# RWKV-7 decode samples: loads one pair of heads ahead, masks and half of the group norms on VectorE

## The chip, the cores and the metric

The kernel runs on one core of one Trainium2 chip. The metric is the device time of one launch in microseconds (us). TensorE (PE) does the matmuls, VectorE (DVE) and ScalarE (ACT) the elementwise work, GpSimd (POOL) a few copies and products, SyncE (SP) issues most of the DMAs. Each engine takes its instructions in order; what is late on one holds everything written behind it on that engine.

## What the reference computes

One step of a two-layer decoder: a gated-DeltaNet mixer and a ConvFFN, then an RWKV-7 mixer and a ConvFFN. The same trunk runs for a prompt (16 meta tokens and 512 tokens) and for 8 samples of 4 tokens that start from given states. The change lies in the RWKV mixer, cut here to what it computes (16 heads of 64):

```
def rwkv_step(S, xs):
    r_t, w_t, k_t, v_t, kk_t, a_t = xs
    sa = einsum('bhvk,bhk->bhv', S, kk_t)
    S = S * w_t - sa[..., None] * (kk_t * a_t) + v_t[..., None] * k_t
    y = einsum('bhvk,bhk->bhv', S, r_t)
    return S, y

S, y = lax.scan(rwkv_step, S0, (r, decay, k, v, kk, a))
mu = mean(y, axis=-1); var = mean(square(y - mu), axis=-1)
y = ((y - mu) * rsqrt(var + GN_EPS)) * ln_w + ln_b      # a norm per head and token
y = y + sum(r * k * r_k) * v                            # bonus
out = (y * gate) @ wo
```

## The kernel before

All 560 tokens (32 of the samples, 528 of the prompt) are columns of one activation matrix; the model width of 1024 is 8 tiles of 128 rows. A product with a weight matrix is done in fp32 by three matmuls of split halves (`hi`, `lo`: L70 on ACT and L71 on DVE split the weights, L115 multiplies).

The recurrence is done in chunks of 64 tokens: products of a chunk's keys (L1353, mask L1360 on DVE), inverses of 32x32 blocks (L1404 to L1418) and their merging (`merge`, 32x32 matmuls L1443 and L1448 with ACT copies L1444 and L1449), then `rec(G)`, which carries the state through the chunks. The 16 heads are two halves, G = 0 and 1, of four pairs of heads each. In a chunk of `rec`, PE, ACT and DVE take turns: L1624 and L1628 on PE, L1629 on ACT, L1633 on PE, L1565 on DVE, L1642 on PE, L1644 on DVE, L1577 on ACT, and L1651 with L1652 for the outputs. SP loads the keys and values of chunk c+2 (L1572, L1573) when chunk c is done. After every second chunk comes `outnorm`, the norm per head: a sum (L1671, DVE), eight ACT operations of 64 columns that take the mean off (L1674), a square (L1676, ACT), a sum (L1677, DVE), an inverse square root of ten small DVE operations, eight ACT operations of 64 columns that scale (L1681), transposes on PE (L1685) and two finishing operations on DVE (L1690, L1691). Each half has six such norms: one for the meta tokens, four for the prompt, one for the samples.

`samples(G)` does the 8 samples for the four pairs of half G, one pair after the other (q = 0 to 3), in one set of buffers: `S0b` (states, for L1739), `S0` (the state to be updated), `vt`, `vx` and `kt` (tokens). Per pair: the loads (L1717 to L1724) and POOL copies (L1731, L1732), then PE L1739 and L1738, ACT L1740, PE L1744, DVE L1565, PE L1749, DVE L1750, two ACT copies (L1752), eight ACT operations that multiply `vx` by a sample's indicator (L1754, the masks), PE L1757, DVE L1758, POOL L1759 and the store (L1760).

`gates` is the gating product, in two halves of 280 columns and 8 tiles each (loads L1535 and L1537, splits L1538 on ACT and L1541 on DVE, matmuls L1547 and L1548, ACT L1549, DVE L1550). The output product has two halves too: `out_half` for G = 0 (tile `osA`, L115; loads of `xs` L1784, sum L1786, store L1787), and the half for G = 1 (`osB`), which comes after all norms and is split by L183 and L184.

The order of all this is set by `Weave`: chains (samples, rec, norms, inverses) and slots (large products, `gates`, `out_half`, in sequence, each behind a gate). A step ends at a `yield a, b, n`: the planner's clock moves by a, and the chain may go on b later. Chains come first; a slot's step is taken when no chain is due. So the yields set the order in which instructions of different chains stand on each engine.

Of the kernel before, what the change touches and what calls it, by code (L numbers as in the profile page):

```python
# [11 lines left out]
AF = mybir.ActivationFunctionType  # L12
# [5 lines left out]
P = 128  # L18
# [1032 lines left out]
def rwkv(E, xp, norm, x_dram, sink):  # L1051
# [4 lines left out]
    with st:  # L1056
# [609 lines left out]
        def outnorm(G, Yt, r, o, n, t, room, lock):  # L1666

            hp = slice(4 * G, 4 * G + 4)
            y = Yt[r].rearrange("p a (u d) -> p (a u) d", u=2)
            mu, var, rs = [ar.tile([P, 8], F32, tag=g, name=g, bufs=2) for g in ("gm", "gv", "gr")]  # L1670
            nc.vector.tensor_reduce(mu[r], y, axis=AX.X, op=ALU.add)  # L1671
            nc.vector.tensor_scalar(mu[r], mu[r], -1.0 / 64.0, None, op0=ALU.mult)
            for u in range(8):
                nc.scalar.activation(y[:, u], y[:, u], AF.Identity, bias=mu[r, u:u + 1])  # L1674
            sq = room[r]
            nc.scalar.activation(sq, Yt[r].rearrange("p a (u d) -> p a u d", u=2), AF.Square)  # L1676
            nc.vector.tensor_reduce(var[r].rearrange("p (a u) -> p a u", u=2), sq, axis=AX.X, op=ALU.add)  # L1677
            nc.vector.tensor_scalar(var[r], var[r], 1.0 / 64.0, 64e-5, op0=ALU.mult, op1=ALU.add)
            rsqrt(E, ar, rs[r], var[r], [P, 8], "gs", r)
            for u in range(8):  # L1680
                nc.scalar.activation(y[:, u], y[:, u], AF.Copy, scale=rs[r, u:u + 1])  # L1681
            yield 0, 6.0, 0
            py = bank([4, n])
            for p in range(4):
                nc.tensor.transpose(py[:, p, :], Yt[r, p, :], E.ident[r, r])  # L1685
            vo, go = v[:, hp, o:o + n], G1[:, hp, o:o + n]
            if n == P:
                py, vo, go = [x.rearrange("p a (c t) -> p a c t", c=2) for x in (py, vo, go)]
            def finish(y):
                nc.vector.tensor_tensor(t, y, go, op=ALU.mult)  # L1690
                nc.vector.tensor_tensor(vo, t, vo, op=ALU.add)  # L1691
            if gated:
                finish(py)
            else:
                nc.scalar.activation(t, py, AF.Copy)
                pending.append(lambda: finish(t))
            if lock is not None:
                ylock[lock] = False
            normed[G] += 1
            yield 0.45, 0.5, 1  # L1700

        def samples(G):
# [9 lines left out]
            nc.gpsimd.memset(kt, 0.0)  # L1712
            nc.gpsimd.memset(vt[up], 0.0)

            def load(p):
                for r in (dn, up):
                    nc.sync.dma_start(out=S0b[r, :, r], in_=I["rwkv_S0"][p, r])  # L1717
                nc.sync.dma_start(out=S0, in_=I["rwkv_S0"][p])
                nc.sync.dma_start(out=vt[dn], in_=vtd[0, :, p, :])
                for hh, c in enumerate((dn, up)):  # L1720
                    nc.sync.dma_start(out=vx[64 * hh:64 * hh + 32], in_=vtd[0, 0:32, p, c])
                    for i in range(2):
                        o = 64 * hh + 32 * i
                        nc.sync.dma_start(out=kt[o:o + 32, c], in_=kbd[0, 64 * i:64 * i + 32, p, c])  # L1724
            for q in range(4):
                p = 4 * G + q
                load(p)
                for i in range(2):
                    x = KR[:, p, 0, i, 0:32].rearrange("p (b t) -> p b t", t=4)
                    zo = 64 * i  # L1730
                    nc.gpsimd.tensor_copy(z[:, zo:zo + 924].rearrange("p (b c) -> p b c", c=132)[:, :, 0:4], x[:, 0:7])  # L1731
                    nc.gpsimd.tensor_copy(z[:, zo + 924:zo + 928], x[:, 7])  # L1732
                yield 0, 2.5, 0
                ps = bank([P])
                for k in range(8):
                    if k == 7:
                        for hh, c in enumerate((dn, up)):
                            nc.tensor.matmul(ps[b, c], lhsT=Ak[dn, 2 * q + hh, 0:32], rhs=vt[dn, c], start=False, stop=False)  # L1738
                    nc.tensor.matmul(ps, lhsT=z[:, P * k:P * k + P], rhs=S0b[:, k, :], start=(k == 0), stop=(k == 7))  # L1739
                nc.scalar.activation(PY, ps, AF.Copy)  # L1740
                yield 2.1, 0.8, 1
                ps = bank([1, P])
                for hh, c in enumerate((dn, up)):
                    nc.tensor.matmul(ps[b, 0, c], lhsT=Ak[b, 2 * q + hh, 0:32], rhs=PY[b, c], start=True, stop=True)  # L1744
                evac_SA(vt[b].unsqueeze(1), ps[b], b, 0, 2 * p, 2)
                yield 0.15, 1.0, 1
                ps = bank([P])
                for hh, c in enumerate((dn, up)):
                    nc.tensor.matmul(ps[a, c], lhsT=Ar[:, 2 * q + hh, 0:32], rhs=vt[:, c], start=True, stop=True)  # L1749
                nc.vector.tensor_tensor(ys[a, q, :], ps[a], PY[a], op=ALU.add)  # L1750
                for hh, c in enumerate((dn, up)):
                    nc.scalar.activation(vx[64 * hh + 32:64 * hh + 64], vt[b, c], AF.Copy)  # L1752
                for b8 in range(8):
                    nc.scalar.activation(vm[:, b8], vx, AF.Copy, scale=ind[:, b8:b8 + 1])  # L1754
                yield 0.15, 1.5, 1
                ps = bank([8, 64])
                nc.tensor.matmul(ps, lhsT=kt, rhs=vm, start=True, stop=True)  # L1757
                nc.vector.tensor_tensor(S0, S0, ps, op=ALU.add)  # L1758
                nc.gpsimd.tensor_tensor(S0, S0, el[:, p, 0:8].unsqueeze(2).to_broadcast([P, 8, 64]), op=ALU.mult)  # L1759
                nc.sync.dma_start(out=O["rwkv_Ss"][p], in_=S0)  # L1760
                yield 0.86, 0.5, 1
            W.chain(outnorm(G, ys, a, 0, 32, KR[:, 4 * G:4 * G + 4, 0, 0, 0:32],
                            f[:, 0:512].rearrange("p (a u d) -> p a u d", a=4, u=2), None))
# [15 lines left out]
        def out_half():  # L1779
            ot = split_half(0, big(E, F32R, "osA", 0))  # L1780
            for m in range(KD):
                t = E.xp.tile([P, T], F32, tag="s", name="xs", bufs=2)[:, :TG]
                for a, b in last_cols(t, x_dram[m]):
                    nc.sync.dma_start(out=a, in_=b)  # L1784
                ps = yield from dense_g(E, [4], ot, TG // 2, n=TG)
                nc.vector.tensor_tensor(half_cols(t), ps[:, :, :TG // 2], half_cols(t), op=ALU.add)  # L1786
                nc.sync.dma_start(out=x2[m], in_=t)  # L1787
# [6 lines left out]
        def seconds():  # L1794
            for i, (r, f) in enumerate(((dn, ev_a), (up, ev_w))):
# [4 lines left out]
        W.slots += [[None, slot(ev_r(m), hook=making(3) if m == 7 else None, split=304)] for m in range(KD)]  # L1800
        W.slots += [[None, slot(ev_v(m))] for m in range(KD)]
        W.slots += [[None, products2()], [lambda: all(ktdone) and len(zdone) == KD and prod_done[1], gates()],
                    [lambda: normed[0] == 6 and bool(gated) and bool(merged[1]), out_half()]]
        W.run()
        assert normed == [6, 6]
        stA.close()
# [233 lines left out]
```

## Time and profile before

| | |
|---|---|
| device time, median of 3 runs (lowest, highest) | 1912.06 us (1908.01, 1916.1) |
| the profiled execution: device time, its span in the trace | 1913.3 us, 1911.3 us |
| mean granted TensorE clock of it | 0.95 of full |
| busy: PE, DVE, ACT, POOL | 1801.1, 1154.5, 803.9, 369.0 us |

Busy time is the union of an engine's instructions. The granted clock is 1.00 at TensorE's full clock of 2.4 GHz and 0.50 at 1.2 GHz; a mean between the two is a share of time at either. The time outside the span is 2.0 us.

### The profile page before, as it was taken

The numbers are of one execution on the slowest core, as the hardware profiler recorded it, in microseconds if no ns is written. First come the engines' busy times: TensorE is split into PE (matmuls) and PEld (weight loads), VectorE is DVE, ScalarE is ACT, GpSimd is POOL, SyncE is SP. The second block draws the span as 40 slices with busy tenths as digits, with TensorE's granted clock in tenths as the row PEclk, the third lists the DMA queues.
The fourth block names the chain that finished last, engine by engine and source line by source line (L and its number), as shares of the span: only waits on it lengthen the run. The fifth ranks groups of instructions, "written<-read, shape, count | busy, mean of one in ns | idle before, by whom it ended". The sixth has DMA issues, their size and how long they took to land.

```text
span 1911.3 us, 36670 instructions
## 1 busy us (share of the span) xinstructions
PE 1801.1 (94%) x14673; PEld 1718.5 (90%) x14673; DVE 1154.5 (60%) x2221; ACT 803.9 (42%) x1779; POOL 369.0 (19%) x616
## 2 busy tenths in 40 slices
PE   7999999999999999998989999799997999999996
PEld 6889998789999999998778997788786999999996
DVE  6698973875555553337787977874555555554223
ACT  4766434442222222222976535554644322222221
POOL 3442403621222220013110000021001111111011
PEclk9999998999999999999898999896898999999998
DMA  4233232433222223444122244332235322223331
GB/s 131 76 91 93 70 90 104 150 122 120 82 89 89 80 87 104 120 155 98 48 70 62 70 117 121 98 91 80 78 102 163 123 89 89 89 88 91 99 109 67
DMA packets 128010, 186.13 MB, mean 97 GB/s; under 512 B 63088, under 2 KB 75376, under 8 KB 127840
## 3 DMA queue, kind: packets, MB, share of 16 engines
q10 hardware_dynamic: 34448, 111.63, 18.7%
q1 hardware_dynamic: 93392, 72.17, 13.0%
q8 instruction: 116, 1.90, 0.4%
q14 instruction: 54, 0.44, 0.1%
HBM read 151.56 MB, written 32.18 MB: 96 GB/s over the span
## 4 chain that ended last, share of the span: by engine, by line
PE 76%; DVE 12%; ACT 3%; DMA 3%; issue 1%; POOL 0%; SPq 0%; DVEq 0%; ACTq 0%
PE pd L115 56%; PE pd L138 3%; PE pg L1353 1%; DVE lo L71 1%; PE pg L1739 1%; PE pg L1628 1%; DVE it L425 1%; PE pg L1624 1%; PE pg L1651 1%; PE pg L1642 1%; DVE tri L1023 1%; PE pg L835 1%; PE pg L1633 1%; DVE cv L593 1%; DMA xd<-xo 1%
## 5 line engine op out<-in xcount | busy, mean ns | idle before, releaser
L115 PE MATMUL pd<-x,hi 128*128 128x280 f32 (+7 forms) x4768 | 837.5, 297 | 23.5 <-ACT hi L70 9.1
L115 PEld LDWEIGHTS pd<-x,hi 128*128 128x128 f32 (+1 forms) x4768 | 695.4, 192 | 30.8 <-ACT hi L70 9.3
L115 PE MATMUL pd<-x,lo 128*128 128x296 f32 (+5 forms) x2384 | 516.4, 297 | 5.6 <-DVE lo L71 5.6
L70 ACT ACTIVATE hi<-raw 128x1024 fp32r<-128x1024 f32 (+3 forms) x218 | 219.8, 1009 | 481.7 <-PE pd L115 447.4
L115 PEld LDWEIGHTS pd<-x,lo 128*128 128x128 f32 (+1 forms) x2384 | 382.9, 192 | 9.9 <-DVE lo L71 6.8
L71 DVE TENSOR_TENSOR lo<-raw,hi 128x1024 fp32r<-128x1024 f32 (+3 forms) x218 | 255.7, 1173 | 219.1 <-ACT hi L70 212.6
L218 POOL TENSOR_TENSOR s<-s,sq 128x560 f32<-128x560 f32 (+2 forms) x30 | 50.8, 1693 | 303.7 <-ACT sq L216 273.9
L304 DVE TENSOR_TENSOR gp<-pd,s 128x528 f32<-128x528 f32 (+1 forms) x44 | 30.8, 701 | 105.9 <-PE pd L115 105.9
L115 PE MATMUL pd<-hl,hi 128*128 128x280 f32 (+1 forms) x448 | 93.5, 290 | 0.0
L115 PE MATMUL pd<-hh,hi 128*128 128x280 f32 (+1 forms) x448 | 93.3, 290 | 0.0
L115 PE MATMUL pd<-hh,lo 128*128 128x280 f32 (+1 forms) x448 | 93.3, 290 | 0.0
L316 ACT ACTIVATE gs<-cv 128x528 f32<-128x528 f32 (+1 forms) x44 | 28.1, 639 | 147.3 <-DVE cv L314 147.3
L115 PE MATMUL pd<-hb,hi 128*128 128x280 f32 (+1 forms) x512 | 85.8, 290 | 0.0
L115 PEld LDWEIGHTS pd<-hb,hi 128*128 128x128 f32 x512 | 72.8, 188 | 0.0
L115 PEld LDWEIGHTS pd<-hh,lo 128*128 128x128 f32 x448 | 70.8, 188 | 0.0
L115 PEld LDWEIGHTS pd<-hh,hi 128*128 128x128 f32 x448 | 70.6, 188 | 0.0
L115 PEld LDWEIGHTS pd<-hl,hi 128*128 128x128 f32 x448 | 70.5, 188 | 0.0
L319 POOL TENSOR_TENSOR gs<-gs,s 128x560 f32<-128x560 f32 (+1 forms) x44 | 60.8, 1382 | 38.1 <-ACT gs L317 38.1
L322 DVE TENSOR_TENSOR h<-pd,gs 128x560 f32<-128x560 f32 (+1 forms) x44 | 32.1, 730 | 57.0 <-POOL gs L319 57.0
L308 POOL COPY fnew<-gp 128x2 f32<-128x2 f32 x44 | 8.1, 185 | 291.5 <-DVE gp L304 291.5
L1023 DVE TENSOR_TENSOR tri<-X 128x4 f32<-128x4 f32 (+26 forms) x124 | 56.0, 451 | 5.2 <-POOL X L1014 2.2
L138 PE MATMUL pd<-os,hi 128*128 128x280 f32 x256 | 52.8, 303 | 2.5 <-ACT os L183 1.9
(539 smaller groups left out, 3039.6 us busy)
## 6 DMA issues: line engine op xcount, KB each, us to landing
raw<-w_up ACTq DMA_DIRECT2D x88, 512.0 KB, 3.3
raw<-w_in ACTq DMA_DIRECT2D x32, 512.0 KB, 3.3
raw<-w_down ACTq DMA_DIRECT2D x32, 512.0 KB, 3.6
raw<-w_down ACTq DMA_DIRECT2D x16, 384.0 KB, 3.0
kbd<-kst SPq DMA_DIRECT2D x18, 256.0 KB, 2.0
KB<-kbd SPq DMA_DIRECT2D x18, 256.0 KB, 3.0
xd<-xo SPq DMA_DIRECT2D x16, 280.0 KB, 2.1
raw<-gdn_out ACTq DMA_DIRECT2D x8, 512.0 KB, 3.3
```

The costliest lines, as they stand in the source:

```text
L70: nc.scalar.activation(hi[:R, :kt, :M], raw[:R, :kt, :M], AF.Copy)
L71: lo_eng.tensor_tensor(lo[:R, :kt, :M], raw[:R, :kt, :M], hi[:R, :kt, :M].bitcast(F32), op=ALU.subtract)
L115: nc.tensor.matmul(ps[b][:M, :c1 - c0] if isinstance(ps, list) else ps[:M, b, :c1 - c0], lhsT=w[:, kk, :M], rhs=x[:, c0:c1], start=(k == 0 ...
L138: nc.tensor.matmul(ps[:, b, :c1 - c0], lhsT=a, rhs=x[:, c0:c1], start=(k == i == 0), stop=(k == len(xs) - 1 and i == 2))
L218: nc.gpsimd.tensor_tensor(self.acc[:, :self.w], self.acc[:, :self.w], sq, op=ALU.add)
L304: nc.vector.tensor_tensor(two(gp[:, m0:]), pm, two(s[:, mo:mo + ml]), op=ALU.mult)
L316: nc.scalar.activation(gs[:, mo:mo + ml], cv[:, m0 - 2:], AF.Silu)
L319: nc.gpsimd.tensor_tensor(gs, gs, s[:, :n_main], op=ALU.mult)
L322: nc.vector.tensor_tensor(two(h), ps[:, :, :hw], two(gs), op=ALU.mult)
L425: nc.vector.tensor_tensor(t.rearrange("p n j -> p j n"), U[:n, i:R, c0:], L[:n, i, i:R].unsqueeze(2).to_broadcast([n, m, k]), op=ALU.mult)
L593: nc.vector.scalar_tensor_tensor(cv, gp[:, i:i + 584], cw[i], cv, op0=ALU.mult, op1=ALU.add)
L1023: nc.vector.tensor_tensor(t.rearrange("p n j -> p j n"), X[:n, i + 1:c1, c0:c1], X[:n, i, i + 1:c1].unsqueeze(2).to_broadcast([n, m1, k]), ...
```

## The change

The samples of a pair no longer load everything at the pair's start. `load` is cut into three: the states (L1717 with the POOL copies), the tokens, and the own state `S0`. For the first pair of a half all three run together, with one `yield 0, 2.5, 0` for the half and none for the others; for the next pair the states are loaded behind the first PE group of the pair before (its readers), the tokens behind L1757 and `S0` behind the store. The eight ACT masks become one DVE operation of 512 columns. In `outnorm`, for G = 1 only, the eight ACT operations for the mean and the eight for the scale become one DVE operation of 512 columns each; G = 0 keeps its ACT operations. The gate of `out_half` no longer asks that all inverses of half 1 are merged. Nothing in the arithmetic changes.

```diff
             nc.vector.tensor_scalar(mu[r], mu[r], -1.0 / 64.0, None, op0=ALU.mult)
-            for u in range(8):
-                nc.scalar.activation(y[:, u], y[:, u], AF.Identity, bias=mu[r, u:u + 1])
+            if G:
+                nc.vector.tensor_tensor(y, y, mu[r].unsqueeze(2).to_broadcast([r.stop - r.start, 8, 64]), op=ALU.add)
+            else:
+                for u in range(8):
+                    nc.scalar.activation(y[:, u], y[:, u], AF.Identity, bias=mu[r, u:u + 1])
...
-            for u in range(8):
-                nc.scalar.activation(y[:, u], y[:, u], AF.Copy, scale=rs[r, u:u + 1])
+            if G:
+                nc.vector.tensor_tensor(y, y, rs[r].unsqueeze(2).to_broadcast([r.stop - r.start, 8, 64]), op=ALU.mult)
+            else:
+                for u in range(8):
+                    nc.scalar.activation(y[:, u], y[:, u], AF.Copy, scale=rs[r, u:u + 1])
...
-            def load(p):
+            def load_states(p):
+
                 for r in (dn, up):
                     nc.sync.dma_start(out=S0b[r, :, r], in_=I["rwkv_S0"][p, r])
-                nc.sync.dma_start(out=S0, in_=I["rwkv_S0"][p])
...
+            def load_tokens(p):
                 nc.sync.dma_start(out=vt[dn], in_=vtd[0, :, p, :])
...
+            def load_own(p):
+                nc.sync.dma_start(out=S0, in_=I["rwkv_S0"][p])
+            for f_ in (load_states, load_tokens, load_own):
+                f_(4 * G)
+            yield 0, 2.5, 0
             for q in range(4):
                 p = 4 * G + q
-                load(p)
...
-                yield 0, 2.5, 0
...
                 nc.scalar.activation(PY, ps, AF.Copy)
+                if q < 3:
+                    load_states(p + 1)
                 yield 2.1, 0.8, 1
...
-                for b8 in range(8):
-                    nc.scalar.activation(vm[:, b8], vx, AF.Copy, scale=ind[:, b8:b8 + 1])
+                nc.vector.tensor_tensor(vm, vx.unsqueeze(1).to_broadcast([P, 8, 64]), ind.unsqueeze(2).to_broadcast([P, 8, 64]), op=ALU.mult)
                 yield 0.15, 1.5, 1
                 ps = bank([8, 64])
                 nc.tensor.matmul(ps, lhsT=kt, rhs=vm, start=True, stop=True)
+                if q < 3:
+                    load_tokens(p + 1)
                 nc.vector.tensor_tensor(S0, S0, ps, op=ALU.add)
...
                 nc.sync.dma_start(out=O["rwkv_Ss"][p], in_=S0)
+                if q < 3:
+                    load_own(p + 1)
                 yield 0.86, 0.5, 1
...
-                    [lambda: normed[0] == 6 and bool(gated) and bool(merged[1]), out_half()]]
+                    [lambda: normed[0] == 6 and bool(gated), out_half()]]
```

PE's order is the same in both kernels up to the first L1757 of half 0, and again from the second half of the output product on. In between, three places matter. The line numbers of the changed kernel are higher: L1739 is L1751 there, L1744 L1758, L1757 L1770, L1685 L1691, L1718 L1740, L1717 L1724, L1719 L1732, L1721 L1734, L1724 L1737, L1760 L1775, L1784 L1801, L1787 L1804.

The first place is PE where the first half of the output product begins; XX and A are the buffers of the samples of half 0 and 1, KB and KR belong to the recurrence. Before:

```order
L1739 MATMUL pg<-A 128x128 x7
L1738 MATMUL pg<-A 32x64 x2
L1739 MATMUL pg<-A 128x128
L1633 MATMUL pg<-KB,A 64x64 x8
L1685 MATMUL pg<-cm,XX 128x32 x4
L1744 MATMUL pg<-A 32x64 x2
L1642 MATMUL pg<-KB 128x128 x4
L1651 MATMUL pg<-KB,A 64x64 x8
L115 MATMUL pd<-osA,hi 128x274 x2
L1624 MATMUL pg<-KB,KR 128x128 x4
```

And with the change:

```order
L1751 MATMUL pg<-A 128x128 x7
L1750 MATMUL pg<-A 32x64 x2
L1751 MATMUL pg<-A 128x128
L1633 MATMUL pg<-KB,A 64x64 x8
L1691 MATMUL pg<-cm,XX 128x32 x4
L1758 MATMUL pg<-A 32x64 x2
L1642 MATMUL pg<-KB 128x128 x4
L1651 MATMUL pg<-KB,A 64x64 x6
L115 MATMUL pd<-osA,hi 128x274
L1651 MATMUL pg<-KB,A 64x64 x2
L115 MATMUL pd<-osA,hi 128x274 x5
L1624 MATMUL pg<-KB,KR 128x128 x4
```

Both times the output product begins right behind the norm of half 0's samples (the L1685, now L1691, that reads XX); but the L1624 that follows is that of rec(1)'s last chunk, the eighth, before, and that of its sixth chunk now, so that three chunks stand between the output product's matmuls.

The second place is PE at the end of that half. Before:

```order
L1685 MATMUL pg<-cm,KB 128x128
L1757 MATMUL pg<-A 128x512
L1685 MATMUL pg<-cm,KB 128x128 x3
L115 MATMUL pd<-osA,hi 128x274 x4
L115 MATMUL pd<-osA,lo 128x274 x2
...
L115 MATMUL pd<-osB,hi 128x274 x2
L1685 MATMUL pg<-cm,A 128x32 x4
L115 MATMUL pd<-osB,hi 128x274 x5
```

And with the change:

```order
L115 MATMUL pd<-osA,hi 128x274 x4
L1642 MATMUL pg<-KB 128x128 x4
L1651 MATMUL pg<-KB,A 64x64 x8
L1770 MATMUL pg<-A 128x512
L115 MATMUL pd<-osA,lo 128x274 x2
L115 MATMUL pd<-osA,hi 128x274 x4
...
L1691 MATMUL pg<-cm,KB 128x128 x4
L115 MATMUL pd<-osB,hi 128x274 x2
L1691 MATMUL pg<-cm,A 128x32 x4
L115 MATMUL pd<-osB,hi 128x274 x5
```

The end of the last chunk (its L1642 and L1651) stands some 20 matmuls of the output product ahead of osB now; before, it stood ahead of nearly all of the output product. The last norm's transposes are the next thing behind those matmuls.

The third place is SP's queue in rec(1), where pairs of half 1 (A) are loaded between the recurrence's loads (KB). Before:

```order
L1572 DMA KB<-kbd 128x512
L1760 DMA out_rwkv_Ss<-A 128x512
L1573 DMA KB<-vtd 64x512
L1724 DMA A<-kbd 32x64
L1718 DMA A<-rwkv_S 128x512
L1572 DMA KB<-kbd 128x512
L1573 DMA KB<-vtd 64x512
L1717 DMA A<-rwkv_S 64x8x64 x2
```

And with the change:

```order
L1775 DMA out_rwkv_Ss<-A 128x512
L1572 DMA KB<-kbd 128x512
L1573 DMA KB<-vtd 64x512
L1740 DMA A<-rwkv_S 128x512
L1724 DMA A<-rwkv_S 64x8x64 x2
L1572 DMA KB<-kbd 128x512
L1573 DMA KB<-vtd 64x512
```

In both kernels the own state's load (L1718, now L1740) stands behind the store of the same buffer and ahead of a chunk's loads; the states' load (L1717, now L1724) has moved ahead of that chunk's loads.

## Rows read from the trace of the kernel before

**Rows 1.** The page: busy us of each engine, share of the span, instructions.

```profile
PE 1801.1 (94%) x14673; PEld 1718.5 (90%) x14673; DVE 1154.5 (60%) x2221; ACT 803.9 (42%) x1779; POOL 369.0 (19%) x616
```

**Rows 2.** Windows: length, PE, PEld, DVE, ACT, POOL busy, clock, DMA share, GB/s.

```profile
1285.30:1301.90 16.60, 11.70 (x124) 9.88 (x123) 13.32 (x33) 11.49 (x34) 1.04 (x1) 0.89 0.27 72
1301.90:1340.00 38.10, 38.10 (x341) 33.01 (x342) 11.19 (x30) 17.61 (x55) 3.93 (x10) 0.55 0.26 74
1340.00:1381.30 41.30, 37.63 (x383) 31.60 (x381) 22.88 (x64) 23.89 (x83) 3.73 (x7) 0.95 0.28 80
1381.30:1394.50 13.20, 13.19 (x71) 11.39 (x71) 4.64 (x14) 6.96 (x27) 0.17 (x2) 0.52 0.11 32
...
1429.50:1450.50 21.00, 10.21 (x62) 8.07 (x61) 13.68 (x36) 10.65 (x33) 1.26 (x3) 0.87 0.54 158
...
1268.70:1450.50 181.80, 161.72 (x1420) 139.40 (x1419) 98.75 (x254) 97.27 (x314) 17.12 (x39) 0.83 0.34 94
```

**Rows 3.** Waits of PE, 1268.7 to 1451 us: total us, times, longest.

```profile
PE pg L1685 <- ACT A L1681: 3.2, 4, 2.7
PE pd L115 <- DVE lo L71: 3.0, 2, 2.3
PE pd L115 <- ACT hi L70: 2.5, 2, 1.7
PE pg L1547 <- ACT gs L1538: 2.2, 1, 2.2
PE pg L1685 <- ACT KB L1681: 2.1, 1, 2.1
```

**Rows 4.** Groups by shape, ACT then DVE then POOL, 1240 to 1451 us.

```profile
L1681 ACT ACTIVATE KB<-KB,gr 128x64 f32<-128x64 f32 x56 | 14.1, 335 | 9.1 <-DVE gm L1672 4.9 <-DVE gr L356 4.2
L1754 ACT ACTIVATE XX<-XX,rc 128x64 f32<-128x64 f32 x32 | 8.2, 334 | 0.0
...
L1565 DVE TENSOR_TENSOR KB<-pg,nw 64x512 f32<-64x512 f32 x12 | 8.3, 694 | 14.7 <-PE pg L1633 14.6
L1786 DVE TENSOR_TENSOR xs<-pd,xs 128x548 f32<-128x548 f32 x8 | 5.8, 726 | 12.1 <-PE pd L115 6.4 <-DMA xs<-xd 5.7
...
L1759 POOL TENSOR_TENSOR A<-A,el 128x512 f32<-128x512 f32 x4 | 4.2, 1044 | 65.5 <-DVE A L1758 65.5
```

**Rows 5.** Timeline of ACT, start of the gates' second half: start, us, instruction.

```profile
1286.36 0.82 ACT L1754 ACTIVATE XX<-XX,rc 128x64 f32<-128x64 f32 x3
1287.08 0.43 ACT L1538 ACTIVATE gs<-g 128x280 fp32r<-128x280 f32 x1
```

**Rows 6.** Timelines of DVE and PE, end of the output product's first half.

```profile
1446.05 0.15 DVE L355 SCALAR_TENSOR_TENSOR rst<-rst,rsi 32x8 f32<-32x8 f32 x1
1446.24 0.15 DVE L356 SCALAR_TENSOR_TENSOR rsi<-rst,rsi 32x8 f32<-32x8 f32 x1
...
1434.65 1.02 PE L1757 MATMUL pg<-A 128*128 128x512 f32 x2
...
1440.96 0.68 PE L115 MATMUL pd<-osA,hi 128*128 128x274 f32 x4
...
1441.73 0.67 PE L115 MATMUL pd<-osA,hi 128*128 128x274 f32 x4
...
1450.50 1.51 PE L115 MATMUL pd<-osB,hi 128*128 128x274 f32 x5 [1.12 <-ACT osB L183]
```

**Rows 7.** Windows within the stretch of the merges.

```profile
1308.50:1339.10 30.60, 30.60 (x248) 26.26 (x245) 9.18 (x27) 15.26 (x50) 3.27 (x6) 0.50 0.24 68
```

**Rows 8.** DMA issues, 1240 to 1451 us: count, KB each, median us to landing.

```profile
KB<-kbd SPq DMA_DIRECT2D x11, 256.0 KB, 3.0
...
out_rwkv_Ss<-A SPq DMA_DIRECT2D x4, 256.0 KB, 2.1
```

**Rows 9.** Timeline of DVE: the last step of two consecutive chunks.

```profile
1367.46 0.68 DVE L1652 TENSOR_TENSOR KB<-pg,KB 64x512 f32<-64x512 f32 x1
...
1375.12 0.68 DVE L1652 TENSOR_TENSOR KB<-pg,KB 64x512 f32<-64x512 f32 x1 [0.35 <-PE pg L1651]
```

More of the change, by code (lines that the diff above doesn't have):

```diff
@@ L1713, in samples @@
             nc.gpsimd.memset(vt[up], 0.0)
-            def load(p):
+            def load_states(p):
                 for r in (dn, up):
                     nc.sync.dma_start(out=S0b[r, :, r], in_=I["rwkv_S0"][p, r])
-                nc.sync.dma_start(out=S0, in_=I["rwkv_S0"][p])
+                for i in range(2):
+                    x = KR[:, p, 0, i, 0:32].rearrange("p (b t) -> p b t", t=4)
+                    zo = 64 * i
+                    nc.gpsimd.tensor_copy(z[:, zo:zo + 924].rearrange("p (b c) -> p b c", c=132)[:, :, 0:4], x[:, 0:7])
+                    nc.gpsimd.tensor_copy(z[:, zo + 924:zo + 928], x[:, 7])
+            def load_tokens(p):
                 nc.sync.dma_start(out=vt[dn], in_=vtd[0, :, p, :])
@@ L1724, in load @@
                         nc.sync.dma_start(out=kt[o:o + 32, c], in_=kbd[0, 64 * i:64 * i + 32, p, c])
+            def load_own(p):
[3 more added lines that the diff above has]
+            yield 0, 2.5, 0
             for q in range(4):
                 p = 4 * G + q
-                load(p)
[L1728 to L1732, printed above, removed]
-                yield 0, 2.5, 0
                 ps = bank([P])
```

## Prediction

> **What bounds the kernel now.** I read the page first: PE is busy 94% of the span [rows 1], so a saving on another engine counts only where PE waits for it, or where PE runs at its lower clock. Then I cut the stretch in which the two orders differ, 1268.7 to 1450.5 us, into windows. Of its 181.8 us PE is busy 161.7, so it waits 20.1; ACT and DVE are each busy a little over half, neither is full [rows 2]. The clock column is the second thing to see there: .55 in the stretch of the merges (1301.9 to 1340), .52 at 1381.3 to 1394.5, .89 and .95 in two others. Busy time times what is missing from 1.00 is the time lost to the lower clock: 38.10 x .45 = 17.1, 13.19 x .48 = 6.3, 37.63 x .05 = 1.9, 11.70 x .11 = 1.3, together 26.6 us (the last window's .87 lies mostly beside waiting and is not counted). So the stretch is 161.7 - 26.6 = 135.1 us of work at full clock, 20.1 of waiting and 26.6 of lower clock. The change leaves the first term alone, since PE does the same matmuls.
>
> The waits by their releaser then say who is late [rows 3]. Sorted by place they are: at the gates and merges about 4.9 us, of which 2.2 is one wait for L1538 on ACT; between chunks about 4.2, of which 2.1 is for the norm's scale L1681 on ACT; inside the first half of the output product 4.7 (parts of the rows on L70 and L71); at its end 6.3 (the 3.2 for the samples' L1681, and the rest of L70 with the split of osB).
>
> **What the change removes and adds.** Eight masks of a pair take 8 x .256 = 2.0 us of ACT (8.2 us for 32), the eight operations of a norm's scale 8 x .252 = 2.0 us (14.1 for 56), and those of its mean as much [rows 4]. ACT loses 8 pairs x 2.0 = 16 us and 6 norms x 2 x 2.0 = 24 us. DVE gets 8 + 12 = 20 operations of 512 columns. The trace has none with these operands; nearest is L1565, 512 columns with a broadcast factor, .694 us, and the longest of the kind is L1786, 548 columns, .726 [rows 4], against .68 for L1652 [rows 9]. I take .69, that is 13.8 us (13.6 to 14.5). The price per operation hardly moves the sum; where it lies does.
>
> *Gates.* L1538, the split that PE waits 2.2 us for, stands on ACT behind the pair's masks: three of them take .82 us just ahead of it, as many more go before with a gate's evacuation between [rows 5]. Without the masks L1538 comes about 1.5 us earlier and the wait falls to some .7. The mask now costs DVE .69 there, where DVE is busy 13.32 of 16.60 [rows 2]; its next work is L1550, which PE reads only through buffers. I take 4.9 down to 3 us; it would stay 4.9 if L1538 were held by its data instead.
>
> *Chunks.* The 2.1 us wait for L1681 comes from ACT doing a norm between a chunk's steps. For G = 1 both runs of eight leave ACT, so this goes. DVE, however, is in the chain of the chunk itself (L1565, L1644), and a norm's or a mask's .69 can stand ahead of either; for about half of 20 operations some .1 to .2 us shows. 4.2 becomes 3 (2 to 6).
>
> *First half of the output product.* The order shows that it now begins with chunk 6 and not with chunk 8, so that three chunks lie between its matmuls. Its own waits came from DVE's L1786, which waits for `xs`, and what stands behind it. With chunks in between, a tile takes about 6 us of PE instead of 3.1 (24 matmuls at .128: in rows 6 six of them take .77), and the loads of `xs` have time. 4.7 becomes 1 (0 to 3). The gate that was loosened costs and gives nothing by itself: in both orders the product begins right behind the norm of half 0's samples.
>
> *Its end.* Here the change takes back. Before, the last chunk stood ahead of nearly all of the output product, and the last norm lay under it. Now PE has only L1757 (1.0 us) and 20 osA matmuls (2.6 us) between the last L1651 and osB [rows 6]. Behind L1651 runs, on DVE nearly alone: L1652 .7, L1671 .7, L1672 .2, the mean .7, on ACT the square .6, L1677 .7, L1678 .2, ten operations of the inverse root spaced .2 (two neighbours of it start .19 apart [rows 6]) 2.0, the scale .7, the transposes .5, L1690 and L1691 1.4, the splits 1.3: 9.7 us. The samples' norm goes through the same queue and adds its own 512-column operations (sum, mean, second sum, scale), the pair's L1758, an L1786 and two weight splits L71, eight times about .7 = 5.6, and .8 of small ones: 16.1 us. Less the 3.6 of cover that is 12.5 us where 6.3 stood (8 to 16).
>
> Waits together: 3 + 3 + 1 + 12.5 = 19.5 against 20.1. So the waits by themselves give about nothing.
>
> *Loads ahead.* The yield of 2.5 per pair goes, so half 0's samples finish sooner against the recurrence; that is what brings the output product forward. The loads themselves were hidden: no long wait of PE ends on a load of the samples [rows 3]. In cover they stand before PE work of several us per pair; without it a landing takes 3 us [rows 8].
>
> *Clock.* The stretch at .52 follows the 2.1 us wait for L1681 at 1381.3 and goes with it. Dense output matmuls now lie in the chunks behind, so I leave 1 of its 6.3 us. The stretch of the merges is the open term. PE is busy all 30.60 of 30.60 us at .50 there [rows 7], so its length is not set by waits inside; it set in after short waits and amid 32x32 and 64x64 matmuls. With the gates' wait gone and the pair's matmuls between gates and merges I expect it to set in later or to end sooner and take 11 instead of 17.1 (3 to 17). The 3.2 us of the two others become 2. Together 14 against 26.6.
>
> **Sum.** 135.1 + 19.5 + 14 = 168.6 against 181.8: 13.2 us less. 1913.3 - 13.2 = 1900.1 for the profiled execution; that one lies 1.2 above the median of the runs, which makes 1899.
>
> **The Trainium skill on the clock.** The rows show PE busy without a gap and yet at the lower level [rows 7]. "TensorE: Matmul & The Clock Gate", Part 1, says "the default state is throttled, and activity releases the throttle". By that rule a busy PE would have its full clock, and with the waits ahead gone all 26.6 us would come back; rows 7 do not agree with that so far, and the measurement decides.
>
> **Rivals.**
>
> *The merges' clock stays as it is* (17.1 us at .50 whatever comes before, since it is held through 30.6 us without a wait). Then the lower clock costs 17.1 + 1 + 2 = 20.1, the sum is 174.7, a gain of 7.1: 1905. For it: rows 7. Chance .30.
>
> *All of the lower clock goes.* 135.1 + 19.5 = 154.6, a gain of 27: 1885. For it: the .52 stretch sets in behind a wait. Against it: rows 7. Chance .12. It is what the rule just named would make of it.
>
> *SP's queue turns the recurrence's loads into the wait* (slower). The own state's load stands behind the store of the same buffer and ahead of a chunk's L1572. From L1757 to that issue pass L1758 .7, POOL L1759 1.04 and a store's landing 2.1, the chunk's load then lands 3.0 later [rows 4, 8]: about 7 us, and the states' load ahead of it adds issue time. Two chunks' ends lie 1375.12 - 1367.46 = 7.7 us apart [rows 9]; with less PE work between, the chunk's load is late. It decides once a chunk takes under about 7 us. At 3 us for each of six pairs and 1.3 us of lower clock behind each (as in the window of the gates' wait, above), it costs 26 us: 1913.3 - 13.2 + 26 = 1926, or 1925 against the median. Against it: chunks get longer through the output product. Chance .08.
>
> *DVE becomes what PE waits for* (slower). If all 13.8 us stood ahead of a waiting PE, the two waits on ACT (4.3) went and the clock stayed, it would be 1913.3 + 13.8 - 4.3 = 1923, or 1922. For it: DVE's 13.32 of 16.60 in one window; against it: DVE is at 54% over the whole stretch [rows 2]. Chance .04. The Trainium skill, "Perfetto Trace Analysis", Optimizing Scalar/DVE Operations, speaks against the change in this way: it would offload from VectorE to ScalarE where VectorE is saturated. The page's rows of this case (60% and 42%) show no saturated VectorE, so the rule has little weight here.
>
> **Chances and range.** The forecast, 1899 (its own range 1893 to 1906), .43; the merges' clock stays .30; all of it goes .12; SP .08; DVE .04; mixtures that come to nothing .03. Within 0.5% means 9.6 us, about what a measurement of this kernel can tell from no change: faster is under 1902.5. Of the forecast's .43 about .33 lies there, of the next .09, of the third .11: .53. Slower are SP and DVE with a little from mixtures, .12 less what the clock gives back: .10. Same .37. The range runs from the third case, 1885, to 1911, where a tail of 15 us and the unchanged clock meet; outside lie the slower cases and a little below, under .2.
>
> **What would show it.** Right: the wait for L1538 under 1 us; no 2 us wait of a transposing L1685 on ACT between chunks; osA's waits about 1 us; at its end 8 to 16 us of waiting for the last norm's DVE operations; the .52 stretch gone; the merges at .50 for clearly less than 30 us. Wrong: the merges at .50 as long as before (then 1905); waits of L1624 or L1642 on SP's loads (then slower); a tail beyond 16 us, or the lower clock setting in behind that tail and running into osB.

## The result: 0.6% faster, and where it shows

Over 20 runs of each, the changed kernel takes 1900.53 us (1891.82 to 1912.51) against 1912.09 (1902.75 to 1924.47): a ratio of 0.994 with a 95% interval of 0.9922 to 0.9958, 11.6 us. In a later set beside other kernels it was 0.9929 (0.9900 to 0.9958).

The profiled execution of the changed kernel is one of its longer ones, 1911.8 us with a span of 1909.7, only 1.6 less than the span before. That does not contradict the median. Most of the kernel has the same instructions in both, and its two profiles differ there as well: the first L1757 of the samples (now L1770) begins at 1274.4 us against 1268.7, before any of the change. So I compare the stretch that did change, from that instruction to the dense osB matmuls (those of the output product's half for G = 1, which follow one another without a wait). Windows of the changed kernel's trace (length, busy time by engine, granted clock, DMA share, GB/s): its parts at the lower clock, then the whole.

```profile
1300.30:1307.00 6.70, 6.70 (x53) 5.59 (x53) 4.34 (x9) 3.20 (x8) 0.00 (x0) 0.50 0.03 7
1327.70:1351.30 23.60, 23.15 (x168) 18.39 (x167) 8.63 (x21) 3.31 (x8) 2.09 (x2) 0.50 0.14 44
1367.40:1371.50 4.10, 4.04 (x19) 3.10 (x20) 3.49 (x13) 0.70 (x3) 0.78 (x1) 0.63 0.03 6
1274.40:1444.40 170.00, 152.74 (x1419) 131.62 (x1418) 110.82 (x273) 61.34 (x162) 17.55 (x39) 0.87 0.36 101
```

The stretch takes 170.0 us where it took 181.8 [rows 2]. PE waits 170.0 - 152.7 = 17.3 us in it against 20.1. The lower clock costs 18.1 us against 27.3 (PE's busy time times what is missing from 1.00, in windows of 1 us; the coarser windows ahead of the prediction gave 26.6). So in these two profiles 2.8 us came from waiting and 9.2 from the clock. ACT's 97.3 us became 61.3, DVE's 98.8 became 110.8.

Waits of PE there, by what released them (total us, times, longest), beside [rows 3]; L1687 is the scale on ACT that was L1681:

```profile
PE pg L1691 <- DVE rsi L351: 8.6, 2, 6.8
PE pd L115 <- ACT osB L183: 4.4, 2, 2.3
PE pg L1691 <- ACT KB L1687: 2.0, 1, 2.0
PE pg L1642 <- DVE KB L1565: 0.9, 2, 0.5
PE pg L1547 <- ACT gs L1538: 0.4, 1, 0.4
```

The wait for the gates' split L1538 fell from 2.2 to .4, the samples' L1681 and both weight splits inside the output product (L70, L71) are gone from the list; in their place stands the end of the half, where PE waits 6.75 us for the last norm on DVE and 2.2 and 2.3 for the osB splits, 11.2 in all. The timeline of PE shows these three waits in brackets:

```profile
1437.55 1.09 PE L1691 MATMUL pg<-cm,KB 128*128 128x128 f32 x4 [6.75 <-DVE rsi L351]
1440.80 0.82 PE L115 MATMUL pd<-osB,hi 128*128 128x274 f32 x2 [2.17 <-ACT osB L183]
...
1444.44 1.51 PE L115 MATMUL pd<-osB,hi 128*128 128x274 f32 x5 [2.25 <-ACT osB L183]
```

### The profile page after: what moved, and what is told of

Same layout as the page of the kernel before. It is cut to its first block, busy times and chain, and to the rows that moved or that the text cites. A ratio compares the mean times of both kernels' runs of the same rounds, so it can differ in the third digit from the quotient of the medians.

```text
span 1909.7 us, 36521 instructions
## 1 busy us (share of the span) xinstructions
PE 1801.9 (94%) x14673; PEld 1717.2 (90%) x14673; DVE 1169.4 (61%) x2241; ACT 766.2 (40%) x1619; POOL 368.3 (19%) x616
## 3 DMA queue, kind: packets, MB, share of 16 engines
q1 hardware_dynamic: 93392, 72.17, 12.9%
## 4 chain that ended last, share of the span: by engine, by line
PE 76%; DVE 12%; ACT 3%; DMA 2%; issue 1%; SPq 0%; DVEq 0%; ACTq 0%
PE pd L115 56%; PE pd L138 3%; PE pg L1353 1%; DVE lo L71 1%; PE pg L1651 1%; PE pg L1628 1%; DVE it L425 1%; PE pg L1642 1%; PE pg L1624 1%; PE pg L1217 1%; PE pg L1751 1%; PE pg L1633 1%; PE pg L835 1%; DVE tri L1023 1%; DVE cv L593 1%
## 5 line engine op out<-in xcount | busy, mean ns | idle before, releaser
L115 PEld LDWEIGHTS pd<-x,hi 128*128 128x128 f32 (+1 forms) x4768 | 695.7, 192 | 34.1 <-ACT hi L70 10.2
L70 ACT ACTIVATE hi<-raw 128x1024 fp32r<-128x1024 f32 (+3 forms) x218 | 219.9, 1009 | 498.5 <-PE pd L115 461.3
L71 DVE TENSOR_TENSOR lo<-raw,hi 128x1024 fp32r<-128x1024 f32 (+3 forms) x218 | 255.0, 1170 | 224.3 <-ACT hi L70 212.9
```

Of the source, the lines that this page charges most:

```text
L70: nc.scalar.activation(hi[:R, :kt, :M], raw[:R, :kt, :M], AF.Copy)
L71: lo_eng.tensor_tensor(lo[:R, :kt, :M], raw[:R, :kt, :M], hi[:R, :kt, :M].bitcast(F32), op=ALU.subtract)
L115: nc.tensor.matmul(ps[b][:M, :c1 - c0] if isinstance(ps, list) else ps[:M, b, :c1 - c0], lhsT=w[:, kk, :M], rhs=x[:, c0:c1], start=(k == 0 ...
```

## The experiments

The three parts that move instructions are called loads (one pair ahead), masks (on DVE) and norms (of half 1, on DVE). "Stretch" is from the first L1757 of the samples to the dense osB matmuls in the kernel's own profile, "waits" what PE is idle in it, "lower clock" the loss worked out as above. The runs were made in three sets, set 1 on one chip, sets 2 and 3 on another, each with runs of the kernel before beside them (35, 27 and 25), so ratios of different sets compare less closely than ratios of one. The loosened gate is in e2, e6, e7 and e12; e3 to e5 and e8 to e11 have the old one. Stretch, waits and lower clock are of one execution each.

| run | set | ratio to before (95%) | median us | stretch | waits | lower clock |
|---|---|---|---|---|---|---|
| before | | 1 | 1912.1 | 181.8 | 20.1 | 27.3 |
| the change | | 0.9940 (0.9922, 0.9958) | 1900.5 | 170.0 | 17.3 | 18.1 |
| e1 gate alone | 1 | 1.0007 (0.9973, 1.0041) | 1910.6 | 180.7 | 20.1 | 26.1 |
| e2 loads alone | 1 | 1.0004 (0.9977, 1.0030) | 1911.2 | 173.5 | 18.9 | 18.1 |
| e3 masks alone | 1 | 0.9984 (0.9952, 1.0015) | 1910.0 | 170.0 | 22.6 | 10.2 |
| e4 norms alone | 1 | 0.9935 (0.9902, 0.9968) | 1893.9 | 158.6 | 16.0 | 6.7 |
| e5 masks and norms | 2 | 0.9896 (0.9856, 0.9935) | 1893.7 | 176.5 | 17.4 | 25.6 |
| e6 loads and masks | 2 | 0.9958 (0.9938, 0.9978) | 1906.1 | 173.3 | 20.3 | 17.1 |
| e7 the change again | 2 | 0.9929 (0.9900, 0.9958) | 1900.8 | 170.0 | 17.5 | 17.9 |
| e8 norms of both halves | 2 | 0.9943 (0.9920, 0.9965) | 1905.1 | 166.6 | 17.3 | 13.8 |
| e9 masks and norms again | 3 | 0.9912 (0.9882, 0.9942) | 1897.3 | 161.8 | 19.1 | 6.5 |
| e10 the same, filled merges | 3 | 0.9942 (0.9921, 0.9964) | 1904.3 | 170.4 | 17.8 | 12.0 |
| e11 before, filled merges | 3 | 0.9961 (0.9937, 0.9985) | 1905.5 | 171.8 | 20.5 | 10.3 |
| e12 loads and norms | 3 | 0.9986 (0.9967, 1.0005) | 1912.2 | 173.6 | 19.9 | 19.2 |

### The parts one by one: e1 to e4

e1 changes one line of the kernel before:

```diff
-                    [lambda: normed[0] == 6 and bool(gated) and bool(merged[1]), out_half()]]
+                    [lambda: normed[0] == 6 and bool(gated), out_half()]]
```

> The kernel before with the gate of the first output half loosened and nothing else. All theories: the instructions of every engine stand in the same order as before, so the ratio is 1.000 within its interval, and the stretch from the first L1757 to osB is again about 182 us with some 20 us of waiting. What it differs by shows how far the granted clock moves one and the same program: I expect the loss to the lower clock in the stretch to lie between 20 and 33 us (26.6 in the profile shown of before).

The ratio is 1.0007, the waits the same 20.1 us, the loss to the clock 26.1 against 27.3. So the gate does nothing that shows, and e1 serves as a second profile of the kernel before: over the merges it has the same stretch at half clock [rows 7].

```profile
1304.00:1334.00 30.00, 30.00 (x241) 25.65 (x239) 8.90 (x27) 14.87 (x48) 3.27 (x6) 0.50 0.22 64
```

e2 has the three `load_` functions and the single yield of the change, with masks and norms left on ACT.

> The kernel before with the samples' loads one pair ahead and nothing else; masks and norms stay on ScalarE. Theory A (the sum on record: the waits balance and the clock gives the gain, which needs the norms on VectorE): the output half starts at chunk 6 or 7, the 2 us wait for L1681 stays, the end of the half waits some 15 us; stretch 178 to 186 us, ratio 0.998 to 1.002. Rival B (the earlier start of the output half, beside the chunks, gives the gain by itself): stretch 168 to 174, ratio 0.994 to 0.996. Rival C (ScalarE's relief gives it): no change or slower, stretch 182 to 190.

No change (1.0004), as theory A had it. Its waits show the price: with the norms on ACT, PE waits 12.9 us for L1681 in three waits, one of 8.6 at the end of the half. The profiled stretch is 173.5, lower than A expected and in rival B's range, which the 12 runs do not follow: one profile's clock is one draw, and from here on the ratios decide and the profiles are read for the waits.

e3 has only this:

```diff
-                for b8 in range(8):
-                    nc.scalar.activation(vm[:, b8], vx, AF.Copy, scale=ind[:, b8:b8 + 1])
+                nc.vector.tensor_tensor(vm, vx.unsqueeze(1).to_broadcast([P, 8, 64]), ind.unsqueeze(2).to_broadcast([P, 8, 64]), op=ALU.mult)
```

> The kernel before with the masks as one VectorE operation and nothing else. Theory A: the wait of L1547 for L1538 falls from 2.2 to under 1 us, the rest stays: stretch 178 to 181, ratio 0.998 to 1.0. Rival B: nothing, 182. Rival C: 8 x 2.0 us of ScalarE show in the waits of the chunks too: waiting falls from 20 to 15 us or less, stretch 173 to 177, ratio 0.995 to 0.997.

0.9984, its interval holds 1. The wait for L1538 fell to 0.8 as expected, but the waits together did not fall (22.6): other ones came at the end of the half (6.0 for the osB split). 16 us less work on ACT by itself is worth at most half a per cent here. Rival C, which read ACT's relief as less waiting (15 us or less), is out by the 22.6; its ratio of 0.995 to 0.997 lies mostly within the interval. The profile also lacks the 30 us at half clock over the merges (the lower clock costs 10.2 us), and yet this execution took 1910.4 us: that one profile does not have them shows no gain.

e4 has only the two branches `if G:` in `outnorm`.

> The kernel before with the norms of half 1 on VectorE and nothing else. The order has 59 osA matmuls (7.6 us) behind the last L1757 and nothing of the recurrence behind those. Theory A: the 2.1 us wait for L1681 goes, and the low clock after it; the end is covered and waits about 4 us; the wait for L1538 stays; stretch 170 to 176, ratio 0.994 to 0.997. Rival B: no gain without the loads, stretch 180 to 184. Rival C: waiting falls from 20 to 12 us or less and the clock's loss stays near 26, stretch 172 to 175.

0.9935: all of the change's gain, by one of its parts. The stretch is shorter than any theory had it, because the half clock over the merges is absent in its profile, which is the shortest of its twelve executions (1888.6 us):

```profile
1265.80:1424.40 158.60, 142.59 (x1419) 124.35 (x1418) 105.26 (x266) 74.61 (x218) 17.12 (x39) 0.95 0.37 108
1302.00:1364.00 62.00, 58.26 (x709) 49.31 (x708) 35.98 (x94) 30.58 (x93) 7.66 (x17) 0.99 0.30 90
```

Rival B (the loads carry the gain) falls with e2 and e4 together. Rival C's number for the waits (12 us or less) did not come either: there are 16.0. That the clock over the merges was full here although the gates' wait of 2.2 us for L1538 was still in place also goes against the reason that I had given for it.

### Leaving one part out: e5, e6, e7, e12

e5 is the change with the loads and the gate as before, e6 with the norms back on ACT, e7 the change itself.

> The changed kernel with the loads as they were before (all of a pair's loads and a yield at its start). The order has 68 osA matmuls behind the last pair's matmul, so the end of the half is covered. Theory A (the norms' 24 us off ScalarE let the clock stay up and remove the 2.1 us wait; loads ahead cost a long uncovered end): faster than the changed kernel, stretch 155 to 162 us, waiting 13 to 16, ratio 0.990 to 0.994. Rival B (the loads ahead are worth something next to the norms): slower than the changed kernel, stretch 172 or more, ratio 0.995 to 0.998.

> The changed kernel with the norms of half 1 back on ScalarE: loads ahead and masks on VectorE stay. Theory A: the gain is gone, the wait for the norm's ScalarE operations at the end of the half is over 10 us, ratio 0.997 to 1.001. Rival B: loads and masks give their part without the norms, ratio 0.993 to 0.996.

> The changed kernel itself beside the others on one chip. Ratio 0.992 to 0.996; in the stretch the same waits as in its first profile (17.3 us, of which some 13 at the end of the half). The loss to the lower clock (18 us there) may move; by theory A it stays under that of the kernel before (26 to 27), by the rival that it is chance it may exceed it.

Without the loads ahead the kernel is at 0.9896, beside 0.9929 for the change in the same set. The intervals overlap, so that this is the better version is likely, not shown; that the loads ahead add something to the norms is not borne out. Without the norms (e6) the ratio is 0.9958, which is rival B's range and not A's: loads and masks give their part without the norms, though neither alone gave anything that can be told. What A said of the waits holds, 14.8 us for L1681, 11.0 of it at once at the end of the half, and 20.3 in all, so the part that they give is not waiting; the lower clock in its profile costs 17.1 us against 26 to 27 before, but in e2's it costs 18.1 without a gain, so that the clock gave it is not shown.

e7 has the same waits as the change's first profile to 0.2 us and the same lower clock in the same place, 24.1 us at half clock from the 53rd us of the stretch on:

```profile
1317.00:1341.10 24.10, 23.36 (x172) 18.48 (x171) 8.74 (x22) 3.68 (x10) 2.09 (x2) 0.51 0.14 49
```

e12 was to complete the table: loads and norms, masks on ACT.

> The changed kernel with the masks back on ScalarE (loads ahead and norms of half 1 on VectorE). Theory A: as the changed kernel within 3 us, since masks alone were worth 0 to 3 us and the loads ahead keep the long end of the output half (waiting there 11 to 16 us): ratio 0.993 to 0.996. Rival (masks count once the norms are gone from ScalarE): 4 us or more slower than the changed kernel, ratio 0.996 to 0.999.

Theory A is wrong here and the rival's number right: 0.9986, against 0.9929 to 0.9940 with the masks moved too. But that the masks count once the norms are gone from ACT is not all of it: with the loads as before, the norms alone gave 0.9935 (e4, in set 1). By these ratios the masks left on ACT cost only beside the loads ahead. With the loads ahead, a pair's masks of half 0 come on ACT just ahead of a norm's scale L1687, for which PE's transposes wait (timelines of e12, ACT and PE):

```profile
1293.73 2.02 ACT L1768 ACTIVATE XX<-XX,rc 128x64 f32<-128x64 f32 x8
1295.65 2.00 ACT L1687 ACTIVATE KB<-KB,gr 128x64 f32<-128x64 f32 x8
...
1296.28 0.47 PE L1691 MATMUL pg<-cm,KB 128*128 128x128 f32 x1 [4.05 <-ACT KB L1687]
```

In the changed kernel that wait is 2.0 us (above): the masks' 2.0 us are the difference. Two microseconds of wait are not the 10 us between the ratios; where the rest comes from is open.

### The clock over the merges: e9, e10, e11

Run times of one kernel spread by 20 us, and the mean granted clock of a run goes with them: e5's six runs go from 1888.4 us at .961 to 1908.9 at .950. The span times the clock hardly moves between kernels: its mean is 1813.5 us before, 1810.9 for the change and 1813.0 for masks and norms, all in set 2, where the run times differ by 14 to 19 us. In set 1 it is 1814.0 before and 1810.6 for e4, with mean times of 1911.0 and 1896.9: of the norms' 14 us about 3 show there, the rest goes with the clock. (A wait at half clock counts as half in that product, so it is a guide, not a sum.)

The merges are not the only place. The changed kernel's two profiles took 1911.8 and 1901.2 us and have the same stretch of 170.0; what sets them apart lies ahead of it, where the instructions are those of before (windows of the first profile and of e7's):

```profile
0.00:1274.40 1274.40, 1208.46 (x9801) 1146.59 (x9801) 851.55 (x1684) 578.08 (x1284) 286.77 (x451) 0.95 0.32 97
```

```profile
0.00:1264.00 1264.00, 1199.17 (x9801) 1139.05 (x9801) 848.40 (x1684) 577.64 (x1284) 286.72 (x451) 0.96 0.31 98
```

e5's profile is its run of 1908.9 us. e9 is the same kernel again, to get a profile of a shorter one.

> Masks and norms without the loads ahead, a second time: its first profile fell among its slower runs (1908.9 of 1888 to 1909) and had 31 us at half clock over the merges. Theory A (one and the same program either has that stretch or not, and this decides some 15 us): the runs again fall into two groups, near 1892 and near 1907; if the profiled one is of the first group, the stretch at half clock over the merges is absent or under 10 us and the stretch to osB is 160 us or less. Rival (the time of a run is not settled there): a profile of either group has the stretch. Ratio 0.988 to 0.993.

It came out at 1893.6 us. One and the same program, over the merges, first e5's window, then e9's:

```profile
1308.50:1339.50 31.00, 31.00 (x251) 26.53 (x249) 12.39 (x31) 8.01 (x20) 3.28 (x6) 0.51 0.19 57
```

```profile
1309.00:1339.00 30.00, 28.93 (x373) 24.58 (x372) 16.12 (x39) 10.99 (x28) 2.75 (x6) 1.00 0.30 90
```

PE gets through 251 matmuls in 31 us at .51 and through 373 in 30 us at 1.00. In the first window it is busy without a gap, in the second it waits 1.1 us: the gapless PE is the one at half speed. The stretches are 176.5 and 161.8 us and the two executions 15.3 us apart, so this stretch accounts for 14.7 of the difference. The waits are alike (17.4 and 19.1), e9 even has more. The rival is out: a profile without it exists. What theory A said of two separate groups of run times shows in e4 (eight runs at 1889 to 1896, four at 1902 to 1911, none between); e9's six runs are spread too evenly to say so.

e11 and e10 put more work of the whole array into the merges, on the kernel before and on masks and norms, two matmuls ahead of each group of sixteen 32x32 ones (L1443, and likewise L1448 into `pu`):

```diff
             py = bank([16, 32])
+            if G:
+                for i in range(2):
+                    nc.tensor.matmul(py[:, 4 * i:4 * i + 4, :], lhsT=E.ident, rhs=mask.rearrange("p (a b) -> p a b", a=4), start=True, stop=True)
             for h in range(16):
```

Their products are overwritten; they do nothing but occupy PE.

> The kernel before with the same added matmuls in half 1's merges and nothing else. Theory A: the stretch at half clock from 1302 to 1340 us of the kernel before shrinks from some 34 us to under 10 and with it some 10 to 15 us of time: ratio 0.992 to 0.997. Rival: ratio 1.001 to 1.003, the added work alone.

> The same, with two added 128x128 matmuls of constants ahead of each of the eight groups of 32x32 matmuls in half 1's merges (their result is overwritten; 16 x 0.27 = 4.3 us of PE at full clock, less what falls into the waits for the ScalarE and VectorE copies there). Theory A (the small matmuls of the merges let the clock fall, more work of the whole array holds it): the low clock over the merges is gone in most runs, the slower group disappears, mean 1890 to 1897, narrower. Rival (the fall does not depend on what PE does there): mean 2 to 5 us above the same kernel without them, two groups as before.

e11 is faster than before with strictly more work: 0.9961 (0.9937 to 0.9985), and its runs are closer together (12 at 1901 to 1915 beside 25 at 1902 to 1924). The gates' wait is still there, 2.2 us, and so are the waits altogether (20.5). What is gone in its profile is the half clock over the merges (the merges' window, then the stretch):

```profile
1301.90:1344.00 42.10, 41.99 (x563) 36.27 (x562) 17.51 (x43) 22.78 (x70) 6.41 (x12) 1.00 0.33 95
...
1270.80:1442.60 171.80, 151.25 (x1452) 130.88 (x1451) 97.33 (x254) 97.85 (x314) 17.93 (x39) 0.91 0.36 100
```

The rival (1.001 to 1.003) is out. That the added matmuls do it as work, and not as a shift in time of what follows them, no run separates.

e10 is the other side of it, and it does not bear theory A out. Its mean is 1903.9 us where A had 1890 to 1897; e9's is 1897.9, so it is 6 us above the same kernel without the added matmuls, where the rival had 2 to 5. Its longest run, 1907.3, is about as long as e9's, 1907.5. Its profile has no 30 us at half clock, but it has 11 us amid the merges and the added matmuls, where e9's has none:

```profile
1301.50:1312.50 11.00, 11.00 (x102) 9.77 (x99) 2.66 (x5) 1.68 (x4) 1.91 (x3) 0.53 0.15 41
```

The added matmuls cost PE about 4 to 6 us (its busy time less the lower clock is 140.5 us, against 136.2 in e9, and 140.9 in e11 against 134.4 before), and here they buy nothing that shows.

### More of the same: e8

e8 is e4 with `if True:` in place of `if G:`, so that half 0's norms move as well.

> The kernel before with the norms of both halves on VectorE (12 norms), nothing else. Theory A, carried on: the five norms of half 0 that lie beside the gates and merges leave ScalarE too (20 us of it), the wait for L1538 stays (it stands behind masks), ratio 0.990 to 0.994, not slower than with half 1 alone. Rival D (VectorE becomes what PE waits for at the gates, where it was 13.3 of 16.6 us busy): 2 to 5 us more waiting for L1550 than with half 1 alone, ratio 0.994 to 0.997.

0.9943, at the edge of rival D's range and no better than half 1 alone (0.9935 in another set), with waits of 17.3 against 16.0: the L1624 waits for L1644 on DVE grew from 0.7 to 2.5 us, those for L1550 did not. So taking 20 more us off ACT gave nothing that shows, and rival D's place was wrong too.

## Why the prediction came out right

**The sum.** 168.6 us were forecast for the stretch and 170.0 measured, twice; 1899 for the kernel and 1900.53 measured. Its two main claims hold: the waits by themselves give little (19.5 forecast, 17.3 measured, from 20.1), and the clock gives most (14 forecast, from 26.6; 18.1 measured, from 27.3, both by windows of 1 us).

That the sum came so close is in part luck. The waits came out 2.2 us lower than forecast and the clock's term 4.1 higher, and most of that cancels. A single profile's clock is also a draw: e5 and e9, one program, differ by 14.7 us in the stretch. And the gain came from another part than the sum had it from: of the 12.6 us that the clock was to give back, the norms had the .52 stretch, 5.3, and the gates' wait (the masks) and the pair's matmuls (the loads) the merges' 6.1. But the norms alone gave all of the gain (e4); masks and loads each alone gave none that shows (e2, e3), and together 0.4% (e6).

**Waits, term by term.** Gates and merges: 3 forecast; .4 for L1538, .2 for L1448 and 2.0 for L1687 are 2.6. The last was not foreseen: it is the same transposing L1691 behind ACT's scale that I had looked for only between chunks, here in a norm of half 0, which stayed on ACT. Chunks: 3 forecast, about 3.4 measured, with 1.8 of it at 1367 us behind DVE's inverse root. Output product: 1 forecast, 0 measured: with three chunks between its matmuls none of its waits is left. End of the half: 12.5 forecast, 11.2 measured. DVE's queue there holds what the prediction listed ahead of the last norm's scale, less one of the two weight splits L71 and the samples' own scale, which comes later; one mean took 1.56 us instead of .7 (last section).

**The clock.** The .52 stretch at 1381 us is gone as said; 4.1 us at .63 stand behind the 1.8 us wait at 1367 and cost 1.5, where 1 was left. The merges were forecast to lose 11 and lost 3.3 + 11.6 = 14.9 (busy time of the first two windows above times .50). Later onset was right; the reason was not. I had put it to the wait ahead of it and the pair's matmuls, but e4 has a full clock there with the wait in place, e11 too, and e5 and e9 are one program with and without the stretch. What holds the clock down there stays open. Fewer waits do not decide it (e9 has more than e5), and added work of the whole array made the kernel before faster (e11), but not the one with masks and norms (e10). Nor is it the 32x32 and 64x64 matmuls alone that run at half clock: in the changed kernel's second window stand products of 128x128 among them (timeline of PE; at 1361.35 eight matmuls of L1624 take 1.16 us):

```profile
1335.32 2.07 PE L1624 MATMUL pg<-KB,KR 128*128 128x128 f32 x8
...
1339.62 1.91 PE L1448 MATMUL pg<-A,TY 32*32 32x32 f32 x32
...
1345.36 2.07 PE L1770 MATMUL pg<-A 128*128 128x512 f32 x2
```

Why the norms of half 1 on DVE raise the kernel's mean clock was not found. Why the kernels with the loads ahead have the stretch later and shorter (23.6 and 24.1 us in the change's two profiles, 27.0 in e12) was not tried either.

**The loads ahead.** The prediction gave them no price, only that they bring the output product forward. The end of the half, 11.2 us of waiting against 9.3 in e9 and 6.6 in e4, is the price they have, and no run shows a gain from them next to the norms (e12, loads and norms, is at 0.9986); next to the masks alone they may have one (e6 against e3, with intervals that overlap).

**The rivals.** "The merges' clock stays as it is" (1905) lies within the spread of the changed kernel's own runs, but neither of its two profiles is of that kind. "All of the lower clock goes" (1885) did not come in any run of the change (lowest 1887.7 us). SP's queue did not become a wait: no wait of PE in the list above ends on a load of the recurrence. DVE did become what PE waits for, but mainly at the end of the half. The Trainium skill, "TensorE: Matmul & The Clock Gate", Part 1, says that activity releases the throttle. The rows do not agree with the forecast that was drawn from it: e5 has PE busy 31.00 of 31.00 us at .51, and the measurement decides.

## What to carry to other kernels

Read the granted clock beside the busy share: a PE that is busy without a gap can be running at half speed (e5, 31.00 of 31.00 us at .51), and there more work on the full array made one kernel faster (e11) and another not (e10). When runs of one program spread, compare the mean clock and the span times the clock before explaining a profile, and take a second profile before a stretch is put down to an edit. One DVE operation with a broadcast (.69 us) in place of eight short ACT operations with a scalar each (2.0) shortens waits only where something waits behind them: with the norms moved PE waits 16.0 us instead of 20.1 (e4), with the masks alone moved 22.6 (e3).

## What the runs showed of the hardware beyond that

One of the new DVE operations took more than twice its time, in both profiles of the change: L1674 on the last chunk's norm, 1.56 us where the others took .68 to .69. It is the only one of its kind that runs beside POOL's L1774 (the timelines of DVE and POOL of the changed kernel):

```profile
1397.89 0.69 DVE L1674 TENSOR_TENSOR KB<-KB,gm 128x512 f32<-128x512 f32 x1
...
1430.01 1.56 DVE L1674 TENSOR_TENSOR KB<-KB,gm 128x512 f32<-128x512 f32 x1
```

```profile
1429.97 1.05 POOL L1774 TENSOR_TENSOR A<-A,el 128x512 f32<-128x512 f32 x1 [1.58 <-DVE gm L1672]
```

POOL starts .04 us earlier and holds 1.05; DVE ends .55 after it. In e9 the order is the other way round: DVE's L1697 starts first, and POOL's product takes 1.43 instead of 1.04 (timelines of e9, DVE, then POOL):

```profile
1413.57 0.67 DVE L1697 TENSOR_TENSOR H<-KR,H 128x512 f32<-128x512 f32 x1
...
1413.72 1.43 POOL L1764 TENSOR_TENSOR A<-A,el 128x512 f32<-128x512 f32 x1 [17.48 <-DVE A L1763]
```

The Trainium skill, "SBUF — State Buffer", Who interferes with whom, says that a VectorE instruction with two inputs in SBUF contends with a GpSimd instruction that reads SBUF, and that the order of issue decides which of the two blocks; these rows agree. It costs .87 us (1.56 - .69) at the one place of this kernel where PE waits for DVE longest, and was in no term of the sum.
